# Row sums of a 67 MB tensor: the block that is contiguous in x moves from the last place to the first, spread over the partitions in groups of four

## The chip, the cores and the metric

The kernel runs on one core of one Trainium2 chip. The time is device microseconds of one execution; three runs of the kernel before gave 160.62, 160.66 and 160.91 us, median 160.66. Profile and trace are of one further execution on the same kind of chip.

## The reference

```python
def reference(x, multiplier):          # x: 32 x 512 x 1024 float32, multiplier 0.5
    return (np.sum(x, axis=-1) * multiplier).astype(np.float32)
```

16,384 rows of 1024 numbers (4 KB each, 67.1 MB in all) are summed and scaled; the output has 16,384 numbers.

## The kernel before, in words

The 16,384 rows are dealt to 128 partitions, 128 rows each, in eight blocks of 16 rows per partition (64 KB per partition, 8.39 MB per block). `B` is 16, `rows` 128, `own` 112.

The first seven blocks come from `x_rows` (line 43): partition p owns the 112 successive rows from 112p, and block b takes its rows 16b to 16b+15. In such a block each partition reads one run of 64 KB, and the runs of neighbouring partitions are 112 rows, 448 KB, apart. The eighth block comes from `x_last` (line 44), the last 2048 rows of x: partition p takes 16 successive rows, so the runs lie side by side, 64 KB apart, and the block is contiguous in x. `res` holds one result per partition and row, 128 columns, in the order of the blocks.

All DMAs are issued by SP, on one queue, by `load` (line 73) or directly. Three buffers of a block each (`buf`, line 52) take turns. The loop over b (line 105) issues the load of block b, which waits, from the fourth on, until the reduction of block b-3 has freed the buffer (line 112). VectorE then sums the block in one instruction (line 117) and scales the sums into `res` (line 123). In block 6 VectorE takes half of the rows, and ScalarE the other half by one activation for each row (`act_row`, line 81).

The eighth block, the tail, is cut (lines 137 to 148): rows 0-7, 8-12 and 13-14 of each partition are three loads into the buffer of block 4, and row 15 comes in two loads of 608 and 416 numbers into a tile of its own, `end`. Their rows are shared by ScalarE (`on_act`, line 155) and VectorE (`dve_sum`, line 90); the very last sums are VectorE's (lines 167 and 170).

Results go out by two stores: an early one (line 150) with the 112 columns of the first seven blocks, issued when these are summed, which runs beside the tail, and the final one (line 175) with the tail's 16 columns. The kernel ends when SP has seen both land (lines 179 and 180).

At build time `start_loads_at_entry` (line 182) moves those loads that wait for nothing, the first three, to the head of the program, ahead of the barrier at which the engines meet. Their order stays; the load of block 0 is the first instruction of SP that the profile shows.

Of the kernel before, what the change touches and what calls it, by code (L numbers as in the profile page):

```python
# [9 lines left out]
def kernel(  # L10
# [13 lines left out]
    nc = tc.nc  # L24
# [4 lines left out]
    P = nc.NUM_PARTITIONS  # L29
# [3 lines left out]
    x_flat = x.flatten_outer_dims()  # L33
    N, D = x_flat.shape
    rows = N // P
    out_flat = out.rearrange("b s -> (b s)")
    mul = float(multiplier)

    B = 16
    n_blocks = rows // B  # L40
    assert N == P * rows and rows == n_blocks * B
    own = rows - B
    x_rows = x_flat[0 : P * own, :].rearrange("(p c) d -> p c d", p=P)
    x_last = x_flat[P * own : N, :].rearrange("(p c) d -> p c d", p=P)
    out_rows = out_flat[0 : P * own].rearrange("(p c) -> p c", p=P)
    out_last = out_flat[P * own : N].rearrange("(p c) -> p c", p=P)

    def sbuf(name, *shape):
        return ctx.enter_context(nc.sbuf_tensor(name, list(shape), fp32)).ap()
# [4 lines left out]
    res = sbuf("res", P, rows)  # L54
    cut = 608
    at = 640
    end = sbuf("end", P, at + D - cut)

    def sem(name):
        return nc.alloc_semaphore(name=name)  # L60
# [5 lines left out]
    def marks(i, engine):  # L66

        s = dve_done if engine == "dve" else act_done
        i.then_inc(s, 1)
        counts[engine] += 1  # L70
        return counts[engine]

    def load(name, dst, src, free=None):
        landed = sem(name)
        i = nc.sync.dma_start(out=dst, in_=src)  # L75
        if free is not None:
            i.wait_op(dve_done, free, "sem-ge")
        i.then_inc(landed, 16)
        return landed

    def act_row(t, r, col):
        return nc.scalar.activation(  # L82
            out=t[:, r, :],
            in_=t[:, r, :],
            func=mybir.ActivationFunctionType.Copy,
            scale=mul,
            accum_out=res[:, col : col + 1],
        )
# [16 lines left out]
    for b in range(n_blocks - 1):  # L105
        c0 = b * B
        t = buf[b % bufs]
        landed = load(
            f"landed{b}",
            t,  # L110
            x_rows[:, c0 : c0 + B, :],
            freed[b - bufs] if b >= bufs else None,
        )
        h = B if b < n_blocks - 2 else B // 2
        nc.vector.wait_ge(landed, 16)
        done = marks(
            nc.vector.reduce_sum(  # L117
                out=sums[:, c0 : c0 + h], in_=t[:, 0:h, :], axis=mybir.AxisListType.X
            ),
            "dve",  # L120
        )
        freed.append(done)
        scaled = nc.vector.tensor_single_scalar(  # L123
            out=res[:, c0 : c0 + h],
            in_=sums[:, c0 : c0 + h],
            scalar=mul,
            op=mybir.AluOpType.mult,
        )
        scaled.wait_op(dve_done, done, "sem-ge")
        early_dve = marks(scaled, "dve")  # L130
        if h < B:
            nc.scalar.wait_ge(landed, 16)
            for r in range(h, B):
                i = act_row(t, r, c0 + r)
            early_act = marks(i, "act")

    c0 = (n_blocks - 1) * B
    t = buf[(n_blocks - 1) % bufs]
    nc.sync.wait_ge(dve_done, freed[n_blocks - 1 - bufs])
    pieces = [(0, 8), (8, 13), (13, 15)]  # L140
    landed = [
        load(f"landed_p{k}", t[:, lo:hi, :], x_last[:, lo:hi, :])
        for k, (lo, hi) in enumerate(pieces)
    ]
    landed_end = [
        load(f"landed_e{k}", end[:, to : to + hi - lo], x_last[:, B - 1, lo:hi])
        for k, (to, lo, hi) in enumerate(((0, 0, cut), (at, cut, D)))
    ]
    nc.sync.wait_ge(dve_done, early_dve)
    early = nc.sync.dma_start(out=out_rows, in_=res[:, 0:own])  # L150
    early.wait_op(act_done, early_act, "sem-ge")
    early_stored = sem("early_stored")
    early.then_inc(early_stored, 16)

    on_act = {4, 5, 6, 7, 11, 12, 14}
    for k, (lo, hi) in enumerate(pieces):
# [15 lines left out]
    done = marks(final, "dve")  # L172

    nc.sync.wait_ge(act_done, late_act)
    store = nc.sync.dma_start(out=out_last, in_=res[:, own:])
    store.wait_op(dve_done, done, "sem-ge")
    stored = sem("stored")
    store.then_inc(stored, 16)
    nc.sync.wait_ge(early_stored, 16)
    nc.sync.wait_ge(stored, 16)  # L180

    def start_loads_at_entry(nc_):
# [61 lines left out]
```

## Time and profile before

| what | us |
|---|---|
| median of three runs | 160.66 |
| span of the profiled execution | 159.43 |
| the load of block 0: issued, landed | 0.0, 21.89 |
| distance of the starts of successive reductions | 19.3 to 19.4 |
| one reduction of a block on VectorE | 17.22 |
| block 6 landed | 137.95 |
| last piece of the tail landed | 157.54 |
| final store: issued, landed | 157.97, 159.39 |

The profiled execution is known by its span; the time of a run covers a little more than the span, 1.23 us where the median is set beside it. Times in the profile count from the first instruction shown, the issue of the first load. A DMA of 128 partitions appears in the trace as 128 packets, one for each run, spread over 16 engines, eight each, and 16 completion marks, one for each engine; it has landed with the last of these.

### The profile page before, as it was taken

How to read it: one execution, taken by the hardware profiler on the slowest of the kernel's cores; microseconds unless marked ns; L12 is line 12 of the kernel's file. 1: busy time of each engine (PE TensorE's matmuls, PEld its weight loads, DVE VectorE, ACT ScalarE, POOL GpSimd, SP SyncE). 2: the span in 40 equal slices, each digit the busy share in tenths (PEclk: the TensorE clock that was granted, in tenths of full speed). 3: DMA queues.
4: the chain of work that ended last, by engine and by line, in shares of the span. 5: the costliest groups of instructions: out<-in, count | busy, mean ns of one | idle time of the engine just before them, and what ended most of it. 6: DMA issues, size and time to landing. Idle time of an engine off the chain costs nothing.

```text
span 159.4 us, 122 instructions
## 1 busy us (share of the span) xinstructions
DVE 119.3 (75%) x35; ACT 17.3 (11%) x31; POOL 0.2 (0%) x4
## 2 busy tenths in 40 slices
DVE  0000059998699978999599995999959999598644
ACT  3000000000000000000000000000000000397954
POOL 0000000000000000000000000000000000000000
DMA  7996996996999979969969969969979799698994
GB/s 263 526 526 263 526 510 280 526 510 280 526 395 395 526 312 477 526 296 493 526 263 526 526 263 526 510 280 526 477 312 526 345 444 526 280 501 364 421 410 145
DMA packets 2016, 67.18 MB, mean 421 GB/s; under 512 B 480, under 2 KB 608, under 8 KB 736
## 3 DMA queue, kind: packets, MB, share of 16 engines
q1 hardware_dynamic: 2016, 67.18, 98.0%
HBM read 67.11 MB, written 0.07 MB: 421 GB/s over the span
## 4 chain that ended last, share of the span: by engine, by line
DMA 76%; DVE 22%; SPq 1%; issue 0%
DMA xb<-in_x_dram 51%; DMA end<-in_x_dram 25%; DVE sums L117 22%; SPq L75 1%; DVE end L92 1%; DVE res L123 0%; DVE res L92 0%
## 5 line engine op out<-in xcount | busy, mean ns | idle before, releaser
L117 DVE TENSOR_REDUCE sums<-xb 128x16 f32<-128x16384 f32 (+1 forms) x7 | 112.0, 16001 | 30.9 <-DMA xb<-in_x_dram 30.9
L82 ACT ACTIVATE xb<-xb 128x1024 f32<-128x1024 f32 x15 | 15.7, 1044 | 137.7 <-DMA xb<-in_x_dram 137.7
L92 DVE CUSTOM_DVE_ANT_0 xb<-xb 128x512 f32<-128x512 f32 x8 | 5.1, 688 | 4.9 <-DMA xb<-in_x_dram 4.9
L82 ACT ACTIVATION_READ_ACCUMULATOR xb<-xb 128x1 f32 x15 | 2.8, 186 | 0.0
L103 DVE MEMSET end<- 128x2 f32 x1 | 0.1, 60 | 2.5 <-PEq L26 2.5
L82 ACT ACT_TABLE_LOAD x1 | 1.3, 1283 | 2.4 <-PEq L26 2.4
L123 DVE TENSOR_SCALAR res<-sums 128x16 f32<-128x16 f32 (+1 forms) x7 | 1.2, 174 | 0.2
L92 DVE CUSTOM_DVE_ANT_0 end<-end 128x304 f32<-128x304 f32 (+1 forms) x2 | 0.9, 426 | 0.1
L92 DVE DVE_READ_ACCUMULATOR2_ANT res<- 128x1 f32 x9 | 0.7, 82 | 0.0
L225 POOL MEMSET const-bfloat16-1.0<- 128x1 bf16 x1 | 0.1, 102 | 0.0
L225 POOL MEMSET const-uint8-127<- 128x1 uint8 x1 | 0.1, 102 | 0.0
L225 POOL MEMSET const-float32-1.0<- 128x1 f32 x1 | 0.1, 99 | 0.0
L225 POOL MEMSET const-float32-0.0<- 128x1 f32 x1 | 0.1, 98 | 0.2 <-issue 0.2
L92 DVE DVE_READ_ACCUMULATOR2_ANT end<- 128x1 f32 x1 | 0.1, 81 | 0.0
## 6 DMA issues: line engine op xcount, KB each, us to landing
xb<-in_x_dram SPq DMA_DIRECT2D x1, 4096.0 KB, 31.2
xb<-in_x_dram SPq DMA_DIRECT2D x1, 2560.0 KB, 36.9
xb<-in_x_dram SPq DMA_DIRECT2D x1, 1024.0 KB, 38.9
end<-in_x_dram SPq DMA_DIRECT2D x1, 304.0 KB, 39.1
end<-in_x_dram SPq DMA_DIRECT2D x1, 208.0 KB, 39.2
xb<-in_x_dram SPq DMA_DIRECT2D x7, 40.8
out_dram<-res SPq DMA_DIRECT2D x1, 56.0 KB, 10.8
out_dram<-res SPq DMA_DIRECT2D x1, 8.0 KB, 1.4
```

What stands on the lines that cost most here:

```text
L75: i = nc.sync.dma_start(out=dst, in_=src)
L82: return nc.scalar.activation(out=t[:, r, :], in_=t[:, r, :], func=mybir.ActivationFunctionType.Copy, scale=mul, accum_out=res[:, col : co ...
L92: return nc.vector.tensor_tensor_reduce(out=row[:, 0:mid], in0=row[:, 0:mid], in1=row[:, mid:], scale=scale, scalar=0.0, op0=ADD, op1=ADD, ...
L103: marks(nc.vector.memset(end[:, at - 2 : at], 0.0), "dve")
L117: nc.vector.reduce_sum(out=sums[:, c0 : c0 + h], in_=t[:, 0:h, :], axis=mybir.AxisListType.X),
L123: scaled = nc.vector.tensor_single_scalar(out=res[:, c0 : c0 + h], in_=sums[:, c0 : c0 + h], scalar=mul, op=mybir.AluOpType.mult,)
L225: nc = _bacc.Bacc("TRN2", target_bir_lowering=False, num_devices=1)
```

## The change

The block that is contiguous in x is loaded first, as block 0, whole. It isn't dealt in the order of the partitions: the 2048 rows are four quarters of 512 rows (2 MB), a quarter has 32 runs of 16 rows, and partition 4g+b takes run g of quarter b. So four neighbouring partitions read in the four quarters, 2 MB apart, and the next four read 64 KB further on in each. The blocks from `x_rows` follow, one place later each; the tail is now the last 16 rows of each partition's 112, cut in the same pieces, so its runs are 448 KB apart. In `res` the columns 0 to 15 are the contiguous block's, the others `x_rows`'s.

The early store becomes two: 96 columns of the `x_rows` blocks, and, behind it on SP's queue, 16 columns of the contiguous block, with a semaphore and a wait at the end of its own. The final store writes 16 numbers (64 B) into each partition's stretch of 112 (448 B) instead of side by side.

```diff
     own = rows - B
+    Q = 4
     x_rows = x_flat[0 : P * own, :].rearrange("(p c) d -> p c d", p=P)
-    x_last = x_flat[P * own : N, :].rearrange("(p c) d -> p c d", p=P)
     out_rows = out_flat[0 : P * own].rearrange("(p c) -> p c", p=P)
-    out_last = out_flat[P * own : N].rearrange("(p c) -> p c", p=P)
+    x_lead = x_flat[P * own : N, :].rearrange("(b g c) d -> g b (c d)", b=Q, c=B)
+    out_lead = out_flat[P * own : N].rearrange("(b g c) -> g b c", b=Q, c=B)
...
         landed = load(
             f"landed{b}",
-            t,
-            x_rows[:, c0 : c0 + B, :],
+            t.rearrange("p c d -> p (c d)") if b == 0 else t,
+            x_lead if b == 0 else x_rows[:, c0 - B : c0, :],
             freed[b - bufs] if b >= bufs else None,
         )
...
-        load(f"landed_p{k}", t[:, lo:hi, :], x_last[:, lo:hi, :])
+        load(f"landed_p{k}", t[:, lo:hi, :], x_rows[:, own - B + lo : own - B + hi, :])
...
-        load(f"landed_e{k}", end[:, to : to + hi - lo], x_last[:, B - 1, lo:hi])
+        load(f"landed_e{k}", end[:, to : to + hi - lo], x_rows[:, own - 1, lo:hi])
...
-    early = nc.sync.dma_start(out=out_rows, in_=res[:, 0:own])
+    early = nc.sync.dma_start(out=out_rows[:, 0 : own - B], in_=res[:, B:own])
...
+    lead = nc.sync.dma_start(out=out_lead, in_=res[:, 0:B])
+    lead_stored = sem("lead_stored")
+    lead.then_inc(lead_stored, 16)
...
-    store = nc.sync.dma_start(out=out_last, in_=res[:, own:])
+    store = nc.sync.dma_start(out=out_rows[:, own - B :], in_=res[:, own:])
...
     nc.sync.wait_ge(early_stored, 16)
+    nc.sync.wait_ge(lead_stored, 16)
     nc.sync.wait_ge(stored, 16)
```

## The prediction

> **What bounds the kernel now.** I read the page first (engines, slices, queues, chain), then the chain of waits in order of time, the windows of single blocks, and the DMA view of the first 4.7 us.
>
> ```profile
> span 159.4 us, 122 instructions
> DVE 119.3 (75%) x35; ACT 17.3 (11%) x31; POOL 0.2 (0%) x4
> q1 hardware_dynamic: 2016, 67.18, 98.0%
> DMA 76%; DVE 22%; SPq 1%; issue 0%
> ```
>
> The one DMA queue keeps 16 engines busy for 98% of the span; VectorE for 75%. The 22% of DVE in the chain is only the way by which a buffer comes free; whether it costs anything shows in the blocks:
>
> ```profile
> 2.55:21.91 19.36, 0.00 (x0) 1.12 (x1) 0.00 (x0) 1.00 1.00 433
> 21.91:41.22 19.31, 17.39 (x2) 0.00 (x0) 0.00 (x0) 1.00 1.00 434
> 41.22:60.56 19.34, 17.39 (x2) 0.00 (x0) 0.00 (x0) 1.00 1.00 434
> ```
>
> These are windows cut at the starts of successive reductions (length, DVE busy, ACT, POOL, clock, DMA share, GB/s). Each 8.39 MB block takes 19.3 us at 434 GB/s with a DMA share of 1.00, and DVE works 17.4 us of it, so it waits some 1.9 us for every block. Loads are bound by the engines that carry them, not by free buffers: two blocks are always queued. The last block, contiguous in x, is the same: block 6 has landed at 137.95 and the final piece at 157.54, which is 19.6 us for the same bytes in five pieces.
>
> So the span is 8 blocks x 19.35 = 154.8 us, plus a start and an end. The end is 1.9 us from the last landing: 157.54 to the span's 159.43 (a VectorE sum of 0.38, the store's issue of 0.34, its landing 1.4 after it was issued). The start is what is left, about 2.6 us, and it has a shape:
>
> ```profile
> DMA  0000000099999090009000000000000000999909
> GB/s 0 0 0 0 0 0 0 0 3347 1116 1116 1116 1116 0 558 0 0 0 558 0 0 0 0 0 0 0 0 0 0 0 0 0 0 0 1116 558 2789 3904 0 558
> DMA packets 32, 2.10 MB, mean 446 GB/s; under 512 B 0, under 2 KB 0, under 8 KB 0
> ```
>
> This is the DMA view of 0 to 4.7 us in slices of 0.1175 us. Bytes are booked where a packet starts; one 64 KB packet in a slice reads 558 GB/s. So six engines start near 1.0 us, two in each of the next four slices, one at 1.68 and one at 2.2. The second group of 16 is the second packet of each engine, thus the end of its first: two at 4.0, one, five, seven near 4.4, and one at 4.63. By the trace's packet records a first packet took 2.42 to 3.34 us, later ones 2.418. The early starters lose 0.6 to 0.9 us; the engine that starts at 2.22 loses nothing more but is last. That spread stays: of the 16 completion marks of block 0 the first comes at 21.27 and the last at 21.89 (0.62 apart), of block 6 at 137.39 and 137.95 (0.56). Every landing waits for the last engine, so **the end of the kernel is set by how late the last engine ends its first packet**, then by 56 times 2.418 us and the tail. Behind 4.63 the next engine is at 4.45.
>
> **The change, part by part.**
>
> *First load.* The same 128 packets of 64 KB, other addresses: neighbouring partitions are 2 MB apart in x inside a group of four, groups 64 KB apart; before, neighbours were 448 KB apart. The first sixteen reads fall into a smaller stretch. Why the first packets are slow the trace doesn't say; if it hangs on where they read, this edit moves it. From both sides: if all engines ended like the earliest (4.01), the path gains 0.62; if every packet took 2.418 from the first start at 1.0, it would gain 1.22, a limit; if the late engine alone joins the others (4.45), 0.18. On the other side, another delay as large as the one seen (0.6 to 0.9) costs 0.6 or more. Against a large effect: the contiguous region was untouched until 117 us, and its first 32 KB packets took 1.213 to 1.224 us, half of 2.418 within 1%, so new addresses alone cost nothing in flight; what is slow is the first packet as such. I take -0.2, the late engine's lead, as the nearest row.
>
> *Its issue.* The source has one more dimension. The ten loads into xb took 0.33 to 0.47 us to issue, this one 0.37; it is on the path, so -0.05 to +0.09; I take +0.03.
>
> *Steady blocks.* Six loads with the old shape and pitch, in the same buffers and waits: 0. The reductions (17.22 us) and the scalings (0.17) have the same shapes, only other columns.
>
> *Tail.* The pieces (32, 20, 8, 2.4 and 1.7 KB per partition) now lie 448 KB apart instead of 64 KB. At 448 KB a 64 KB packet takes 2.418 us (27.1 GB/s per engine), at 64 KB pitch a 32 KB one 1.213 (27.0): no difference for large ones. Small ones are not in the trace at the wide pitch. Per engine they are 8 each of 0.309, 0.098 and 0.069 us; a tenth on the last two is 8 x 0.167 x 0.1 = 0.13, the spread of the 8 KB packets (0.309 to 0.321) 8 x 0.012 = 0.10. So 0 to +0.23; a gain is excluded as they already run near the rate of large ones. I take +0.05, nearer to the large packets' row.
>
> *Stores.* One more DMA, 128 pieces of 64 B, and one more wait. SP issues it at about 147.3 for 0.35 us; nothing is behind it on SP until the wait for ScalarE ends at 157.4:
>
> ```profile
> SPq L174 <- ACT xb L82: 10.1, 1, 10.1
> SPq L180 <- DMA out_dram<-res: 1.1, 1, 1.1
> ```
>
> Thus 9.7 us of cover. On the queue it stands behind the tail loads and the early store, whose last packet ended at 157.28; 8 packets per engine of 8 to 11 ns end at 157.38, and the final store's packets start at 158.81: 1.4 us of cover. Without cover it would be 0.35 + 0.09. The new wait stands ahead of the one for the final store and passes 1.5 us before it: 0. The early store's pieces shrink from 448 to 384 B, beside the same cover. The final store writes 64 B pieces at a pitch of 448 B instead of side by side. From last packet to completion it took 0.37 us (159.02 to 159.39), the early store at that pitch 0.50 (157.28 to 157.78); so 0 to +0.13 on the path; I take +0.03, as size and count stay.
>
> **Sum:** -0.2 + 0.03 + 0.05 + 0.03 = -0.09 on the span of 159.43, thus 159.34. The profiled execution is known by its span alone; the median of the three runs, 160.66, lies 1.23 above it. With that kept the time is **160.55**.
>
> **The rivals.** About 0.2% (0.32 us) is what a measurement of this kernel can tell from no change; the three runs lie between 160.62 and 160.91.
>
> *The start tightens (faster).* The first sixteen reads lie close together and all engines end their first packet like the earliest, at 4.01: -0.62, with the other terms -0.5, 160.15. For it: the delays differ from engine to engine although their work is the same. Against it: new addresses later cost nothing.
>
> *The start worsens (slower).* The sixteen first reads, all begun at once in a stretch of some 2 MB, hold one another up for as long again as now (0.6), so the last first packet ends at 5.2 instead of 4.63: 160.66 + 0.6 + 0.1 = 161.35. It decides from 0.3 us on, a last first packet behind 4.95. For it: all first packets but one are already late when they start together. Against it: they end within 0.6 us of each other wherever they begin.
>
> *The lead block runs below the engines' rate (slower).* Its source has 32 outer steps, its target 128 partitions; if the pieces fall on the engines so that they get in each other's way, or the 2 MB steps do, each 1% of rate costs 0.19 us, and at half the rate it is +19.3, 180.0. It decides from 1.7% on. Against it: two pitches, 448 and 64 KB, have given the same 27 GB/s per engine. The Trainium skill (DMA: Bandwidth & Descriptors, Latency and other measured facts) speaks for it: copies with 2 MiB between the rows of partitions ran at 164 GB/s where padded ones gave 214. By that the lead block would take 19.35 x 214/164 = 25.2 us, an estimate of +5.9 and 166.6; the trace has no such pitch, so no row bears this out or denies it. That page's section on the descriptor swizzle gives each engine two groups of four partitions, which would put the 2 MB steps inside one engine's sequence and not between engines in step; then its rule would not bite.
>
> *It doesn't do what it says:* the first packets are late for a reason that no address changes (then 160.7 to 160.9 by the small terms). This belongs to "no change", and is why I keep that likeliest.
>
> **How the numbers follow.** No measurable change 0.40 (160.55; own range 160.35 to 160.95). Start tightens 0.33 (159.8 to 160.3). Start worsens 0.16 (161.0 to 161.5). Lead block slow 0.11 (161.0 to 180). The range 159.8 to 161.5 leaves out most of the last case and a little of the second, about 0.14. Faster by over 0.2%: 0.33; within: 0.40; slower: 0.27.
>
> **What would show it.** Start: in the DMA view of 0 to 4.7 us the sixteen second packets; the last near 4.45 by the forecast, all near 4.0 for a gain, behind 4.95 for a loss. Rate: the first reduction starts at 21.9 now; over 22.3 with a tight start means a slow lead block, and the distance to the second reduction stays 19.3. Tail: from the start of the reduction of block 6 (137.97) to the final store's issue (157.97) are 20.0 us; each 0.05 more is the tail's. End: 1.46 us from that issue to the end of the span. The prediction is wrong if the first landing moves by over 0.3 us, or if a small piece at the wide pitch costs more than a tenth.

## The result

The changed kernel takes 161.50 us (median of four runs, 161.42 to 161.59) where the kernel before takes 160.66 (160.62 to 160.91). The ratio is 1.0047, with a 95% interval of 1.0033 to 1.0061: slower. The two medians are 0.84 us apart, the ratio makes it 0.75, and the spans of the two profiled executions, from which all that follows is read, differ by 0.74.

### The profile page after: what moved, and what is told of

The parts are those of the page before. It is cut to its first block, busy times and chain, and to the rows that moved or that the text cites. A ratio compares the mean times of both kernels' runs of the same rounds, so it can differ in the third digit from the quotient of the medians.

```text
span 160.2 us, 124 instructions
## 1 busy us (share of the span) xinstructions
DVE 119.3 (74%) x35; ACT 17.3 (11%) x31; POOL 0.2 (0%) x4
## 3 DMA queue, kind: packets, MB, share of 16 engines
q1 hardware_dynamic: 2160, 67.18, 97.7%
## 4 chain that ended last, share of the span: by engine, by line
DMA 76%; DVE 22%; SPq 1%; issue 0%
DMA xb<-in_x_dram 51%; DMA end<-in_x_dram 24%; DVE sums L118 22%; SPq L76 1%; DVE end L93 1%; DVE res L124 0%; DVE res L93 0%
```

## The profile after

The page of the changed kernel, the same four lines as were shown of before:

```profile
span 160.2 us, 124 instructions
DVE 119.3 (74%) x35; ACT 17.3 (11%) x31; POOL 0.2 (0%) x4
q1 hardware_dynamic: 2160, 67.18, 97.7%
DMA 76%; DVE 22%; SPq 1%; issue 0%
```

The span is 0.74 us longer (160.17 against 159.43), the busy times are the same, and the share of the queue falls from 98.0 to 97.7%. So no compute engine does more. The share of the queue is of a longer span: 97.7% of 160.17 us is 156.5 us, 98.0% of 159.43 was 156.2. The packets thus take about 0.3 us more for each of the sixteen DMA engines, and each stands idle some 0.4 us longer. The windows between the starts of the first, second and third reduction show where this is not:

```profile
22.55:41.90 19.35, 17.39 (x3) 0.00 (x0) 0.00 (x0) 1.00 1.00 434
41.90:61.24 19.34, 17.39 (x2) 0.00 (x0) 0.00 (x0) 1.00 1.00 434
```

The blocks take the time they took. But the first reduction starts at 22.55 instead of 21.91: 0.64 of the 0.74 us are lost before the first block has landed. The rest is in small change: from there to the reduction of block 6 it is 116.11 us (116.06 before), from this to the final store's issue 20.04 (20.00), and from the issue to the end, the last of these windows, 1.47 (1.46):

```profile
138.66:158.70 20.04, 14.89 (x22) 16.03 (x30) 0.00 (x0) 1.00 0.94 395
158.70:160.17 1.47, 0.00 (x0) 0.00 (x0) 0.00 (x0) 1.00 0.06 6
```

The start, in two views. The chain of waits (start, length, what) opens with SP's issue of the first load:

```profile
0.00 0.67 SPq L76
0.67 0.05 issue
0.71 41.16 DMA xb<-in_x_dram
```

That issue took 0.37 us before:

```profile
0.00 0.37 SPq L75
0.37 0.05 issue
0.42 40.78 DMA xb<-in_x_dram
```

The DMA view of 0 to 5.8 us, in slices of 0.145 us, where one 64 KB packet that starts in a slice reads 452 GB/s; first one line of the kernel before in these slices, then the changed kernel:

```profile
GB/s 0 0 0 0 0 0 1808 1808 904 1356 452 452 0 0 0 452 0 0 0 0 0 0 0 0 0 0 0 904 452 2260 3164 452 0 0 0 0 0 0 0 0
```

```profile
DMA  0000000000999900009000000000000999999000
GB/s 0 0 0 0 0 0 0 0 0 0 2712 2712 904 452 0 0 0 0 452 0 0 0 0 0 0 0 0 0 0 0 0 452 452 1808 2260 1356 904 0 0 0
DMA packets 32, 2.10 MB, mean 362 GB/s; under 512 B 0, under 2 KB 0, under 8 KB 0
```

The first packets start at 1.50 us instead of 1.00, and the second ones, thus the ends of the first, run up to 5.26 instead of 4.63. That is +0.63, the loss of the first landing (21.89 to 22.52). What makes the last packet last is different, too, by the packet records. Before, it was the packet that began late (at 2.22) and took 2.42 us. Now it is one that began at 1.55 and took 3.72 us, while the late starter (2.65, for 2.43 us) is done by 5.08. The stores stay covered: the new store of SP is issued at 148.03 and takes 0.60 us where a plain one takes 0.35, but SP then waits 9.5 us for ScalarE all the same.

```profile
SPq L178 <- ACT xb L83: 9.5, 1, 9.5
SPq L185 <- DMA out_dram<-res: 1.0, 1, 1.0
```

## What was asked

Two things changed at the start at once: the form of the first DMA (its source has two steps, 32 and 4, where all others have one) and its addresses. Theory F says that the form costs the time, by its issue. Theory A says that the addresses do, by slower first packets. Theory T, for completeness, puts it on tail and stores. Most runs are small edits of the first load; where block 0 then sums other rows, the expectation says so.

## Form, addresses, tail: four runs

**Contiguous first, in plain form.**

```diff
-    x_lead = x_flat[P * own : N, :].rearrange("(b g c) d -> g b (c d)", b=Q, c=B)
+    x_lead = x_flat[P * own : N, :].rearrange("(p c) d -> p (c d)", p=P)
```

(and `out_lead` likewise)

> The contiguous block is still first and the tail still lies 448 KB apart, but partition p takes run p, so that the first load has the same plain form as the others (128 runs, one step). Theory F (the loss is the form of the first DMA, whose source has two steps, 32 and 4: SP issued it in 0.67 us instead of 0.37 and the first packet started at 1.50 instead of 1.00): issue 0.37, first packet at 1.0, first landing near 21.9, time 160.6 to 160.8. Theory A (the loss is in the addresses: first packets that read a small contiguous stretch are slower): first landing stays near 22.5, time 161.3 to 161.6. Theory T (tail and stores): the time stays near 161.4 with the first landing back at 21.9.

Measured: 160.80, ratio 1.0003 (0.9994 to 1.0012). The issue takes 0.37 us; the DMA view, again in slices of 0.145:

```profile
GB/s 0 0 0 0 0 0 904 2260 1808 1356 452 452 0 0 0 0 0 0 0 0 0 0 0 0 0 0 0 0 1356 3616 2260 0 0 0 0 0 0 0 0 0
```

Starts from 1.01, ends up to 4.48. The moved tail and the third store are in this kernel too, so theory T is out: with the block's new place they cost at most 0.12%, the upper end of the interval. What costs is the way in which the block is dealt to the partitions, not that it comes first.

**The form alone.**

```diff
+    x_3d = bass.AP(x_flat.tensor, 0, [[4 * own * D, 32], [(own + 1) * D, 4], [1, B * D]])
-            x_rows[:, c0 : c0 + B, :],
+            x_3d if b == 0 else x_rows[:, c0 : c0 + B, :],
```

> The kernel before with one edit: the first load's source is written with two steps, 32 times 1792 KB and 4 times 452 KB, so that it has the form of the changed kernel's first load and nearly the old addresses. The four partitions of a group read 0, 1, 2 and 3 rows further on than they should, so the sums of block 0 are of neighbouring rows. Tail and stores are those of before. Theory F: issue 0.67, first packet at 1.5, first landing 22.4 to 22.6, time 161.2 to 161.5. Theory A: issue may change, but the first landing stays at 21.9 and the time at 160.6 to 160.8. Theory T: 160.66.

Measured: 161.10, ratio 1.0022 (1.0013 to 1.0032). The chain opens with

```profile
0.00 0.63 SPq L77
0.63 0.06 issue
```

and the first packets run from 1.41 to 5.11 (slices of 0.145 again):

```profile
GB/s 0 0 0 0 0 0 0 0 0 1808 2260 904 904 452 904 0 0 0 0 0 0 0 0 0 0 0 0 0 0 0 452 1356 2712 1808 452 452 0 0 0 0
```

So the form costs 0.26 us of issue, another 0.15 between the end of the issue and the first packet (0.78 instead of 0.62), and some 0.35 us of time by the ratio. That is theory F, but only about half of the loss: it had been expected to bring all of it.

**The two first loads exchanged.**

```diff
-        c0 = b * B
+        c0 = (B, 0)[b] if b < 2 else b * B
-            x_lead if b == 0 else x_rows[:, c0 - B : c0, :],
+            x_lead if b == 1 else x_rows[:, c0 - B : c0, :],
```

> The changed kernel with its first two loads exchanged: block 0 comes from the 112 rows of each partition in plain form, the contiguous block in its groups of four is block 1; results in the same columns, stores and tail as in the changed kernel. Theory F: the two-step load is issued while block 0 is on its way, so its 0.3 us are hidden; first landing 21.9, second 41.2, time 160.65 to 160.85. Theory A: if only the first packets suffer from such addresses, also near 160.7; if the block as a whole is slower, the second landing is late. Theory T: near 161.4.

Measured: 160.74, ratio 1.0000 (0.9992 to 1.0009); landings at 21.93 and 41.26. The same load with the same form and addresses costs nothing when another is on its way. Both costs belong to the start alone.

**Two steps, but 128 outer ones on both sides.**

```diff
+    x_3d = bass.AP(x_flat.tensor, 0, [[own * D, P], [(B // 2 + 1) * D, 2], [1, B // 2 * D]])
```

> The kernel before with the first load in two runs of 32 KB per partition, 8 rows each, the second run starting one row late (rows 0 to 7 and 9 to 16, so the sums of half of block 0 are of neighbouring rows). Source and target both have 128 outer steps and a second dimension of 2; 256 packets of 32 KB. It asks what in the form costs. If the number of dimensions does: issue 0.6 to 0.7, first landing 22.4 to 22.6, time 161.2 to 161.5. If it is that the source has 32 outer steps and the target 128: issue 0.37 to 0.45, first landing 21.9 to 22.0, time 160.6 to 160.8. Theory A: 160.66.

Measured: 160.96, ratio 1.0013 (1.0005 to 1.0022); the issue takes 0.43 us, the first packet starts at 1.08. So a further dimension alone costs 0.06 us of issue; the rest of the 0.26 must come with what else the form has, 32 outer steps of the source against 128 partitions of the target. The ratio lies between the two expectations, and its 32 KB packets make a comparison of the ends uncertain; it settles only the issue.

## The other half: is it there, and which addresses?

Four more runs on one chip: the changed kernel again, and three patterns of two steps. "Groups" are the 32 groups of four neighbouring partitions, "steps" the distance within a group. In the changed kernel groups are 64 KB apart and steps are 2 MB.

> The changed kernel as it is, beside the next three on one chip. The form alone cost 0.22% of the 0.47%. If the remainder is real, the ratio is 1.004 to 1.006, and the first packets end on average 0.2 us later than in the run with the form alone (there 2.32 us after subtracting 2.42 for the packet itself, here 2.56). If the remainder was scatter of one profile and four timings, the ratio is 1.002 to 1.003.

> The changed kernel with its two-step form and the contiguous stretch, but with the runs in natural order: partition 4g+b reads run 4g+b (moved by b rows to keep the two steps, so the sums of block 0 are of neighbouring rows and the stores are the changed kernel's). Theory O (the remainder comes from the order: groups of four over quarters 2 MB apart, so that the 16 engines begin 64 KB apart): the remainder goes, ratio 1.002 to 1.003, as with the form alone. Theory N (the remainder comes from a near stretch together with the form): ratio 1.004 to 1.006.

> The kernel before with the first load's source in two steps over the far rows: partition 4g+b reads the run of owner 32b+g, 448 KB from group to group and 14 MB from one of the four to the next (sums of block 0 land in other partitions' places). Tail and stores of before. Theory O, if what matters is that neighbouring groups are near and the four far apart in any measure: ratio 1.004 to 1.006. If it is the 64 KB and 2 MB of the changed kernel: 1.002 to 1.003.

> The changed kernel with its order of quarters, but each run 68 KB after the last instead of 64 and the quarters 2176 KB apart instead of 2048 (the runs skip a row, so the sums of block 0 are of other rows). Theory P (the remainder comes from steps that are powers of two, so that the engines begin at like addresses): it goes, ratio 1.002 to 1.003. Otherwise 1.004 to 1.006.

The edits are the steps in the source:

```diff
+ near, in order:   (P * own - 3) * D,      [[Q * B * D, 32], [(B + 1) * D, Q], [1, B * D]]
+ far quarters:     0,                      [[own * D, 32], [32 * own * D, 4], [1, B * D]]
+ padded quarters:  (N - P * (B + 1)) * D,  [[(B + 1) * D, 32], [32 * (B + 1) * D, Q], [1, B * D]]
```

Measured: changed kernel again 1.0048 (1.0036 to 1.0061); in order 1.0023 (1.0014 to 1.0032); far quarters 1.0060 (1.0047 to 1.0073); padded 1.0094 (1.0079 to 1.0110). The remainder is real, and hangs on the order of the addresses: in the repeat the first packets end on average 0.20 us later than with the form alone (2.52 against 2.32 after subtracting 2.42), as expected. Its last one ends at 5.36, 0.10 from the first profile's 5.26, so the last end of one execution stands for its kernel to 0.1 us at best. Theory P fell: steps that aren't powers of two were worse, not better. The padded run also shows best how the time comes about. Its DMA view of 0 to 6.3 us (one packet reads 416 GB/s here):

```profile
GB/s 0 0 0 0 0 0 0 0 0 3329 2081 0 832 0 0 0 0 416 0 0 0 0 0 0 0 0 0 416 832 1248 2497 832 416 0 0 0 0 0 416 0
```

Fifteen engines end their first packet by 5.07, one at 6.11, and the whole kernel, 160.9 us of span, is later by what that one engine is later.

## Groups or steps

**Cut into four plain loads**, one for each quarter (`t[k::Q]` from `x_lead[:, k, :]`):

> The changed kernel with its first load cut into four plain ones, one for each quarter and its 32 partitions (every fourth), at the same addresses; all four are waited for together. No source has two steps. SP issues four instead of one, each near 0.35 us, but the first can start after 0.37. Theory F with theory O: the first packets start at 1.0 again and the order of addresses within an engine changes, so the last end is set by the fourth load: its issue ends near 1.4 us, and whether the 16 engines share the 32 packets of a load evenly isn't known; ratio 1.000 to 1.003 if evenly, above 1.005 if not. If the remainder hangs on the near addresses alone whatever the form, 1.002 to 1.004.

Measured: 161.40, ratio 1.0045 (1.0032 to 1.0057). The expectation had the issue wrong: these loads of 32 partitions take 0.57 to 0.59 us each, not 0.35, so nothing is gained; the last first packet ends at 5.22. Which part of such a load makes its issue long, the 32 outer steps or the target's every fourth partition, is open. The first packet starts 0.78 us after the end of the first issue, as with two steps, although no source here has two. So the later start isn't a matter of the second step as such.

**Near groups, small steps** (`[[B * D, 32], [5 * D, Q], [1, B * D]]`):

> The changed kernel with its two-step form and its 64 KB from group to group, but only 20 KB instead of 2 MB between the four partitions of a group (the runs overlap, so the sums of block 0 are of other rows). Three runs with 2 MB or more between the four had late first packets (last end 5.26 to 6.11 us), two with 68 and 452 KB had not (5.03 and 5.11). Theory S (large steps within a group make them late): last end 4.9 to 5.15, ratio 1.0015 to 1.003. Theory G (groups 64 KB apart make them late): last end 5.25 or more, ratio 1.004 to 1.006.

Measured: ratio 1.0060 (1.0046 to 1.0074), last end 5.32. Theory S fell; theory G stands.

**Near groups in plain form, and the two factors crossed:**

```diff
+ plain, 64 KB groups:         P * own * D, [[4 * D, P], [1, B * D]]
+ 448 KB groups, 20 KB steps:  0,           [[own * D, 32], [5 * D, 4], [1, B * D]]
+ 256 KB groups, 2 MB steps:   0,           [[4 * B * D, 32], [512 * D, 4], [1, B * D]]
```

> The kernel before with the first load in plain form, but only 16 KB from partition to partition, so that groups of four lie 64 KB apart as in the changed kernel (the runs overlap; the sums of block 0 are of other rows; tail and stores of before). Theory G (the remainder comes from groups 64 KB apart, form or not): issue 0.37, first packets at 1.0, their mean excess over 2.42 is 0.85 to 0.9 instead of 0.64, ratio 1.001 to 1.0025. If the remainder needs the two-step form as well: excess near 0.65, ratio 0.9995 to 1.0005.

> The kernel before with the first load in two-step form, groups 448 KB apart and 20 KB between the four of a group (runs of a group overlap; other rows are summed in block 0). Groups 448 KB apart with 14 MB steps had late first packets (last end 5.78, ratio 1.006). Theory G in the sense that the distance of groups decides, 448 KB being a bad one too: ratio 1.004 to 1.007. If there it was the 14 MB steps: 1.002 to 1.003, as with the form alone.

> The kernel before with the first load in two-step form, groups 256 KB apart and 2 MB between the four of a group (runs overlap between groups' quarters; other rows are summed in block 0). Groups 256 KB apart with 68 KB steps had no late first packets (last end 5.03, ratio 1.0023). Theory G: 1.002 to 1.003 again. Theory S (steps of 2 MB and more make them late, beside near groups): 1.004 to 1.006.

Measured: 1.0030 (1.0020 to 1.0041); 1.0069 (1.0056 to 1.0082); 1.0033 (1.0021 to 1.0044). The second and third, DMA views of 0 to 5.8 us (452 GB/s a packet):

```profile
GB/s 0 0 0 0 0 0 0 0 0 2712 2260 904 0 452 452 0 0 452 0 0 0 0 0 0 0 0 0 0 0 0 452 2260 904 1356 452 452 452 452 0 0
```

```profile
GB/s 0 0 0 0 0 0 0 0 0 2260 2712 904 904 0 0 0 452 0 0 0 0 0 0 0 0 0 0 0 0 0 0 3164 2712 904 452 0 0 0 0 0
```

Both start alike at 1.4. With groups 448 KB apart the ends trail from 4.4 to beyond 5.5; with 256 KB they stand within 0.45 us of each other, although the steps are 2 MB. And plain near groups, whose first packets start at 1.00 after an issue of 0.37, still end at 5.18. So the distance of the groups costs by itself, without the form: 0.30% here, beside 0.22% for the form alone; together 0.52%, and the changed kernel has 0.47%. The DMA view of the plain near groups:

```profile
GB/s 0 0 0 0 0 0 452 4068 2260 452 0 0 0 0 0 0 0 0 0 0 0 0 0 0 0 0 0 904 0 1356 2260 904 904 452 0 452 0 0 0 0
```

The loss of the plain near groups is a little above what was expected for it (to 1.0025). The ratio of the groups 256 KB apart lies between the two expectations, and its interval reaches into both; what speaks for theory G there is the last end, 4.96, beside 5.11 for the form alone.

**Which distances?** Three more, all plain (`[[r * D, P], [1, B * D]]` with r of 8, 32 and 20):

> The kernel before with the first load in plain form, 32 KB from partition to partition, so groups of four 128 KB apart (runs overlap; other rows are summed in block 0). So far groups 256 and 1792 KB apart began on time (ratio 1.000 plain), groups 64, 68 and 448 KB apart late (1.003 for 64 plain). If nearness decides with a bound between 64 and 256 KB this lies between, 1.0005 to 1.002; if only whole multiples of 256 KB are good, 1.002 to 1.006.

> The same with 128 KB from partition to partition, groups 512 KB apart. If multiples of 256 KB are good: ratio 0.999 to 1.001. If the two good distances were so by accident, anything up to 1.006.

> The same with 80 KB from partition to partition, groups 320 KB apart: farther apart than the good 256 KB, but no multiple of it. If multiples of 256 KB are what is good: ratio 1.002 to 1.006. If distances from 256 KB on are good and 448 KB was bad for another reason: 0.999 to 1.001.

Measured: 1.0006 (0.9997 to 1.0015), 1.0002 (0.9993 to 1.0011) and 1.0024 (1.0015 to 1.0032). Nearness isn't it: 320 KB is late, 128 KB is not. Nor is it that 128 KB is too near and whole multiples of 256 KB are needed, as one of the expectations had it. The run with 512 KB, on time, and the run with 320 KB, whose runs don't overlap (0 to 5.8 us, 452 GB/s a packet):

```profile
GB/s 0 0 0 0 0 0 0 4068 2260 0 452 0 0 452 0 0 0 0 0 0 0 0 0 0 0 0 0 0 1808 2260 2712 452 0 0 0 0 0 0 0 0
```

```profile
GB/s 0 0 0 0 0 0 904 2712 1808 0 452 452 452 0 452 0 0 0 0 0 0 0 0 0 0 0 0 0 1356 2260 1356 904 452 452 452 0 0 0 0 0
```

The runs whose first load is one load of whole 64 KB packets (without the repeat of the changed kernel and without the exchanged loads, whose first load is that of before):

| first load | groups, steps (KB) | issue | first packets end by | ratio |
|---|---|---|---|---|
| before, plain | 1792, 448 | 0.37 | 4.63 | 1 |
| contiguous first, plain | 256, 64 | 0.37 | 4.48 | 1.0003 |
| plain | 128, 32 | 0.37 | 4.63 | 1.0006 |
| plain | 512, 128 | 0.38 | 4.53 | 1.0002 |
| plain | 320, 80 | 0.37 | 4.94 | 1.0024 |
| plain | 64, 16 | 0.37 | 5.18 | 1.0030 |
| two steps, the form alone | 1792, 452 | 0.63 | 5.11 | 1.0022 |
| two steps, in order | 256, 68 | 0.66 | 5.03 | 1.0023 |
| two steps | 256, 2048 | 0.63 | 4.96 | 1.0033 |
| two steps, **changed kernel** | 64, 2048 | 0.67 | 5.26 | 1.0047 |
| two steps | 64, 20 | 0.67 | 5.32 | 1.0060 |
| two steps | 448, 14336 | 0.64 | 5.78 | 1.0060 |
| two steps | 448, 20 | 0.61 | 5.82 | 1.0069 |
| two steps, padded | 68, 2176 | 0.67 | 6.11 | 1.0094 |

In plain form the first packets end by 4.63 at 128, 256, 512 and 1792 KB from group to group ("on time"), and later at 64 and 320. With two steps they end by 5.11 at 256 and 1792 KB, which is on time for that form, and later at 64, 68 and 448. So all on-time distances are multiples of 128 KB and none of the late ones is. The average over the sixteen engines parts the same way: first packets end on average at 4.29 to 4.32 us where a plain load is on time and at 4.43 and 4.49 where it is late; with two steps at 4.66 to 4.74 and at 4.82 to 5.00. That fits every row, but it is a rule read off eight distances, most of them tried in one form only, and what lies behind it no run shows. Where the first read begins isn't it: the loads with 128, 320, 448 and 512 KB begin at the same address, two of them on time and two late. The span less the last end is 154.8 to 154.9 us in every row, over 1.6 us of difference in the ends.

**A small load ahead**, into a tile of its own, tried on the kernel before:

> The kernel before with a load of 64 B per partition issued ahead of block 0, into a tile of its own that nothing uses. It asks what the 0.65 us are that a first packet takes beyond 2.42. Theory W (the first packet that an engine carries is slow, whatever it is): the small packets take the delay, the first 64 KB packets start near 1.4 and take 2.42, the last ends at 4.2 to 4.4, ratio 0.997 to 0.999. Theory L (each load needs that long from its issue until its data flow): the last first packet ends at 4.9 to 5.0, ratio 1.0015 to 1.0025, by the issue of 0.35 us.

Measured: 161.26, ratio 1.0032 (1.0020 to 1.0045). The 64 KB packets start from 1.49 on and the last of the first sixteen ends at 5.11. They are still 0.79 us slower than 2.42 on average, though each engine has carried eight small packets by then. Theory W fell; the excess belongs to the first large packets, and an issue ahead of them is only lost time, a little more than I had put on it.

No version beat the kernel before: the best three, contiguous first in plain form, the exchanged loads and groups of 512 KB, are the same within 0.1%.

## Why the prediction was wrong

*What bounds the kernel* held, and more sharply than it was put: the end is the last engine's end of its first packet plus a constant, in seventeen kernels (the rows of the table, and the runs with the exchanged loads, the four plain loads and the small load ahead). Small slips in the prediction's sums change nothing: 159.34 and 1.23 make 160.57 and not 160.55, what is left for the start is 2.7 us and not 2.6, and behind an engine's first packet come 55 more of 2.418 us and not 56.

*The first load* is the term that failed. It was put at -0.2: the one late engine was to join the others, because the first reads lie closer together. With the issue's +0.03 the last first packet was to end 0.17 earlier; it ended 0.63 later, and the sign that the prediction named for itself, a first landing moved by over 0.3 us, was seen (21.89 to 22.52). Less the issue's 0.30, +0.33 stands where -0.2 was put. The runs showed two things in its place. Part of it comes with the form, a first packet that starts later behind the issue; the other part with the addresses: groups 64 KB apart end their first packets later, by themselves 5.18 against 4.63 at an unchanged issue. The row on which "new addresses alone cost nothing in flight" rested was right (the exchanged loads cost nothing), but it spoke of packets in flight and not of the first ones. And reads close together gave no gain where they were dealt in plain form: contiguous first, in plain form, took 1.0003.

*Its issue* was the second: +0.03, with an upper end of 0.09 taken from ten loads that all have one step. It was 0.30 (0.37 to 0.67), and the first packet came a further 0.20 later (1.50 less 1.00 less 0.30). None of those rows had two steps; their spread bounded the wrong thing. The Trainium skill (DMA: Bandwidth & Descriptors, Latency and other measured facts) gives about 0.6 us to the first byte of a DMA issued by SP. Counted from the end of the issue, the plain form agrees (0.62 to 0.64 to the first packet), and the two-step form takes 0.77 to 0.83.

*Steady blocks, tail and stores* held: 0 was +0.05, +0.05 was +0.04, +0.03 was +0.01. The covers named for the third store were there.

*The rivals.* "The start worsens", at 0.16, is what happened, at nearly its price: 5.2 and 161.35 were written down, 5.26 and 161.50 measured. That the price fits is luck. About half of the loss came with the form of the load, which this rival doesn't have; and for the other half it named the small stretch in which the first reads lie, where the runs show groups 448 KB apart later still and groups 128 KB apart on time. "The first packets are late for a reason that no address changes" fell as well: at an unchanged issue the addresses alone moved their last end from 4.63 to 5.18. "The lead block runs below the engines' rate" did not occur: after the first, the packets of the changed block take 2.418 to 2.420 us like all others. The Trainium skill's row on 2 MiB between partitions (DMA: Bandwidth & Descriptors, Latency and other measured facts) would have given 166.6 by the prediction's estimate. It did not bite here: the changed kernel took 161.50, and with steps of 2 MB and groups of 256 KB the run can't be told from the two others with two steps and on-time distances (1.0033 against 1.0022 and 1.0023, intervals overlapping).

*The forecast* of 160.55 had the wrong sign, and the time was at the edge of the range.

## What to carry to other kernels

In a kernel that streams at the DMA engines' rate from the first packet to the last, nothing later makes up for a late start: read the end of the last engine's first packet, since every tenth of a microsecond there is a tenth at the end. Give the first DMA the plainest form there is, one step over the partitions, and put any load with two steps or an odd dealing behind it, where it cost nothing here (1.0000). The plain form isn't enough by itself: plain loads began late too, with groups 64 or 320 KB apart, so read the start of each dealing. A spread of durations bounds only operations of the same form.

## What the runs showed of the hardware

- A load or store whose DRAM side steps 32 by 4 takes SP 0.60 to 0.67 us to issue, a plain one mostly 0.33 to 0.47; a second step beside 128 outer ones takes 0.43. The plain load issued right behind a first load of that form takes 0.57 to 0.58 instead of 0.42. The first packet of a load that steps 32 by 4 also starts later after the end of the issue, 0.77 to 0.83 against 0.62 to 0.64 us; so does that of a load of 32 partitions with one step (0.78).
- The first 64 KB packets of a stream take up to 2.0 us more than the 2.418 of the later ones (4.37 with groups of 448 KB and far quarters), and how much depends on the distance in x from one group of four neighbouring partitions to the next: on time at 128, 256, 512 and 1792 KB, late at 64, 68, 320 and 448 KB. The step within the four made no difference that the runs resolve (at 448 KB 1.0060 and 1.0069, at 64 KB 1.0047 and 1.0060, at 256 KB 1.0023 and 1.0033, each pair with overlapping intervals). Which partitions an engine carries is not in the trace; the Trainium skill (DMA: Bandwidth & Descriptors, The descriptor swizzle) says that in a transfer to 128 partitions each engine carries two groups of four neighbouring ones, which would fit this.
- Small packets sent ahead don't take the excess away (0.79 us on average behind them, 0.64 without).
